# Moving score matmuls and probability products inside one attention step of an encoder kernel

## The chip, the cores and the metric

The kernel runs on one core of one Trainium2 chip. The metric is the device time of one execution in microseconds (us); a lower number is better. Engines are called by the names of the profile: PE (matrix multiply), PEld (its weight loads), DVE (vector), ACT (activations), POOL (GpSimd) and SP (which only issues transfers here).

## The reference

One encoder layer runs over two token sequences, a prompt of 512 tokens and a sample of 2048. The layer is a norm, an input projection, a mixer made of a pooling half and an attention half, an output projection, and a feed-forward part with a short convolution. Only the attention matters for this change:

```
def attend(q_blk):
    s = jnp.einsum('bqhd,bkhd->bhqk', q_blk, k_full).astype(jnp.float32) * scale
    p = jax.nn.softmax(s, axis=-1).astype(v.dtype)
    return jnp.einsum('bhqk,bkhd->bqhd', p, v)
```

There are 8 heads, 96 values in a query or key, 64 in a value, and no mask: every query sees every key of its own sequence.

## The kernel before, in words

The kernel first projects all tokens and leaves queries, keys and the pooled half in HBM, with the values in SBUF. Then comes the attention, then the output projection, and last the feed-forward part. All fp32 operands of matmuls are cut into two fp16 parts, a high and a low one.

The attention is a list of **units**. A unit is one head and one block of queries: 256 queries in the prompt (16 wide units, 0 to 15) and 128 queries in the sample (128 narrow units, 16 to 143). A narrow unit has 16 tiles of 128 keys, so its scores fill 4 PSUM banks of 512 columns, 4 tiles to a bank. Scores stand transposed, keys on the partitions. One narrow unit i goes through these pieces:

- `st_scores` (L935): 3 matmuls (high by high, high by low, low by high) for each key tile, 12 to a bank, 48 to a unit.
- `st_max` (L951): DVE reduces a bank over its 4 tiles to 128 columns; `st_fold` (L971) folds the results of the first three banks into one, and bank 3 has its own.
- `st_T` (L978): two PE transposes put the folded maximum and the maximum of bank 3 side by side in a PSUM tile called x, of which there is only one.
- `st_redT` (L991): DVE reduces x to the maximum of each query and cuts it in two parts (three instructions).
- `st_rep` (L1005): one more PE transpose into x, and ACT copies the negative to SBUF. This is **the copy of the maximum**, tile mr (L1013).
- `st_r1` (L1016): four matmuls of 512 columns add that negative maximum to the four banks.
- `st_exp` (L1030): ACT takes the exponential of each bank into pf (fp32).
- `st_hi` (L1037) casts pf to fp16 (ph), on ACT or on DVE; `st_lo` (L1051) lets POOL form the rest pl = pf - ph.
- `st_pv` (L1056): **the products**, 16 tiles with 2 matmuls each (ph of 129 columns, pl of 65 columns). Their output lies in the x tile of a later unit, so they can't start before that unit's copy of the maximum has left x, and x can't be written anew before the products' output has been copied away.
- `st_out` (L1073): ACT copies the products' output (L1082); `st_out2` (L1087) normalizes and stores once in four units.

The order on every engine is written out by hand. The program takes one step for each i, and a string of letters says which pieces the step issues. Each engine works through its own instructions in exactly that order, so a piece that waits holds up what stands behind it on its engine. The letters that matter: `r` adds the maximum to the banks of unit i, `e0` and `e1` are the exponentials of banks 0 to 2 and of bank 3, `A` and `B` the two halves of a unit's products, `o` the copy of their output, `L` the scores of bank 3 of unit i+1, `a b c` the scores of banks 0 to 2 of unit i+2, `x y z` their maxima, `F` the fold, `M` the maximum of bank 3 of unit i+1, `T`, `d` and `R` the three stages of the maximum of unit i+1 (transposes, reduction, transpose back with its copy), `h0 h1` casts on ACT, `f2 f3` casts on DVE, `l0` to `l3` the rests on POOL. Before the change:

```
A=lambda i: run(st_pv, i - 1, 0),
B=lambda i: run(st_pv, i - 2, 1),
h1=lambda i: run(st_hi, i, 1),
f2=lambda i: run(st_hi, i, 2, 0.5, dve),
f3=lambda i: run(st_hi, i, 2.5, 1.5, dve),
ORDER = "r e0 B L o e1 a M f2 T d b c h0 R h1 l0 l1 A x y f3 l2 l3 z F q"
```

So the first half of the products of unit i-1 stood behind `R`, and its second half at the head of the next step. The banks of scores come from a ring of seven PSUM banks (`bank`, L930); a bank comes free when the exponential of the unit that held it has been taken. From step 36 on, two steps of every four also issue a piece of `prep_w_out` (L818), which scales and cuts the weights of the output projection; two of these pieces go through the x tile on PE and DVE.

Of the kernel before, what the change touches and what calls it, by code (L numbers as in the profile page):

```python
# [48 lines left out]
def encoder(ctx, tc, ins, outs, seq_names=("x_prompt", "x_sample")):  # L49
    nc = tc.nc  # L50
    act, dve, pool, pe = nc.scalar, nc.vector, nc.gpsimd, nc.tensor
# [160 lines left out]
    with tp("wA", 1) as wA, tp("pA", 2) as pA, tc.manual_schedule():  # L212
# [142 lines left out]
        sg, _ = pow2_scale(amr[:, 0:4], 0)  # L355
# [12 lines left out]
        sw, _ = pow2_scale(amr[:, 4:5], 15)  # L368
# [97 lines left out]
        swu, _ = pow2_scale(amr[:, 5:6], 15)  # L466
# [217 lines left out]
        skv, _ = pow2_scale(amr[:, 6:8], 15)  # L684
        swk, swv = skv[:, 0:1], skv[:, 1:2]
        swp, _ = pow2_scale(amr[:, 10:11], 15)
# [6 lines left out]
        swq, _ = pow2_scale(qm, 15)  # L693
# [87 lines left out]
        k = NC - 1  # L781
# [31 lines left out]
    f2 = wC.tile([P, 8], F32, name="f2")  # L813
# [84 lines left out]
    with tp("pB", 2) as pB, tp("psX", 1, "right", space=PSUM) as psX, \  # L898
# [27 lines left out]
        state = {}  # L926
# [3 lines left out]
        def bank(name):  # L930

            nbank[0] += 1
            return (psS if nbank[0] % 7 else psT).tile([P, 512], F32, name=name, tag="st")

        def st_scores(i, b):  # L935
            u = units[i]
            s, h, w = u["s"], u["h"], u["w"]
            if u["first"] and b == 0:
                j = [x for x in range(len(heads)) if heads[x][0] is s and heads[x][1] == h][0]
                if j + 1 < len(heads) and j > 0:  # L940
                    load_head(*heads[j + 1])
            kt, qt = loaded[(s["base"], h)]
            st = u["st"][b] = bank(f"st_{i}_{b}")
            t0, t1 = u["banks"][b]
            for t in range(t0, t1):
                for n, (x, y) in enumerate(THREE):
                    pe.matmul(st[:, (t - t0) * w:(t - t0 + 1) * w], kt[:, x, t * P:(t + 1) * P],  # L947
                              qt[:, y, u["q0"]:u["q0"] + w], start=n == 0 and t == t0, stop=n == 2,
                              skip_group_check=True)
# [106 lines left out]
        def st_pv(i, part):  # L1056
            u = units[i]
            s, h, nq, nkt, w = u["s"], u["h"], u["nq"], u["nkt"], u["w"]
            if part == 0:
                op = state.get(("x", i + 2 if i >= wide - 1 else wide if i >= wide - 3 else NU)) or bank(f"op_{i}")  # L1060
                u["op"] = op[:, :2 * 129].rearrange("p (j c) -> p j c", j=2)
            op = u["op"]
            k0 = s["base"] // P
            jobs = [(j, t) for j in range(nq) for t in range(nkt)]
            n = len(jobs)
            parts = PARTS
            for j, t in jobs[parts[part] * n // 16:parts[part + 1] * n // 16]:
                c0 = t * w + j * P
                pe.matmul(op[:, j, 0:129], u["ph"][:, c0:c0 + P], V[:, k0 + t, h, 0:129], start=t == 0, stop=False)  # L1069
                pe.matmul(op[:, j, 64:129], u["pl"][:, c0:c0 + P], V[:, k0 + t, h, 64:129], start=False,  # L1070
                          stop=t == nkt - 1)

        def st_out(i):  # L1073
            u = units[i]
            s, h, nq, op = u["s"], u["h"], u["nq"], u["op"]
            qi = u["q0"] // P
            grp = qi // 4
            key = ("t", s["base"], h, grp)
            if key not in state:
                state[key] = pB.tile([P, 4, VW], F32, name=f"t_{i}", tag="tacc")  # L1080
            tt = state[key]
            act.activation(tt[:, qi % 4:qi % 4 + nq, 0:129], op[:, 0:nq, 0:129], AF.Copy)  # L1082
            if (qi + nq) % 4 == 0 or (qi + nq) * P == s["S"]:
                n = qi % 4 + nq
                pool.tensor_tensor(out=tt[:, :n, 64:128], in0=tt[:, :n, 64:128], in1=tt[:, :n, 0:64], op=ALU.add)
# [23 lines left out]

        NU = len(units)  # L1110
        prep = prep_w_out(pB, lambda: state["x", max(k for n, k in (x for x in state if x[0] == "x"))])
        PARTS = [0, 8, 16]
        wide = sum(u["nq"] > 1 for u in units)
        ps_first = {}

# [6 lines left out]
        def run(fn, k, *a):  # L1122
            if 0 <= k < NU:
                fn(k, *a)

        def some(fn, k, bs):
            if 0 <= k < NU:
                for b in bs:
                    if b < len(units[k]["banks"]):
                        fn(k, b)  # L1130

        step = dict(
            r=lambda i: some(st_r1, i, range(4)),
            e=lambda i: some(st_exp, i, range(4)),
            e0=lambda i: some(st_exp, i, range(3)),
            e1=lambda i: some(st_exp, i, [3]),
            A=lambda i: run(st_pv, i - 1, 0),
            B=lambda i: run(st_pv, i - 2, 1),
            E=lambda i: run(st_pv, i - 2, 0),
            L=lambda i: some(st_scores, i + 1, [3]),  # L1140
            a=lambda i: some(st_scores, i + 2, [0]),
            b=lambda i: some(st_scores, i + 2, [1]),
            c=lambda i: some(st_scores, i + 2, [2]),
            t=lambda i: some(st_scores, i + 3, [0]),
            u=lambda i: some(st_scores, i + 3, [1]),
            M=lambda i: some(st_max, i + 1, [3]),
            x=lambda i: some(st_max, i + 2, [0]),
            y=lambda i: some(st_max, i + 2, [1]),
            z=lambda i: some(st_max, i + 2, [2]),
            F=lambda i: run(st_fold, i + 2),  # L1150
            h0=lambda i: run(st_hi, i, 0),
            h1=lambda i: run(st_hi, i, 1),
            f1=lambda i: run(st_hi, i, 1, 1, dve),
            f2=lambda i: run(st_hi, i, 2, 0.5, dve),
            f3=lambda i: run(st_hi, i, 2.5, 1.5, dve),
            l0=lambda i: some(st_lo, i, [0]),
            l1=lambda i: some(st_lo, i, [1]),
            l2=lambda i: some(st_lo, i, [2]),
            l3=lambda i: some(st_lo, i, [3]),
            T=lambda i: run(st_T, i + 1),  # L1160
            d=lambda i: run(st_redT, i + 1),
            R=lambda i: run(st_rep, i + 1),
            o=lambda i: run(st_out, i - 2),
            q=lambda i: run(st_out2, i - 3))
        START = ["a b x y", "a b T d t x u y R", "r e T d t R x y u f1 l1 h0 l0",
                 "r e T d t R x y u f1 l1 h0 l0", "r e T d E B R x y f1 l1 h0 l0 o q"]
        ORDER2 = "r e E B o T d a b x R f1 l1 y h0 q l0 c z F"
        TURN = {wide - 1: "r e L a M x T d b h0 f1 R y l0 l1 E B o c z F q",
                wide: "r e0 E B L o e1 a M f2 T d b c h0 R h1 l0 l1 A x y f3 l2 l3 z F q"}
        ORDER = "r e0 B L o e1 a M f2 T d b c h0 R h1 l0 l1 A x y f3 l2 l3 z F q"  # L1170
        for i in range(-2, NU):
            order = START[i + 2] if i + 2 < len(START) else TURN.get(i, ORDER2 if i < wide else ORDER)
            for x in order.split():
                step[x](i)
            if i >= NU // 4 and i % 4 in (0, 1):
                next(prep, None)
            if i == NU - 8:
                for _ in prep:
                    pass
                c_load_m(0)  # L1180
                c_load_m(1)
        todo = [(0, 0), (0, 1), (1, 0), (1, 1), (0, 2), (1, 2), (0, 3), (1, 3)]
        st_pv(NU - 2, 1)
        st_pv(NU - 1, 0)
        st_out(NU - 2)
        st_pv(NU - 1, 1)
        st_out(NU - 1)
        for m in range(2):
            if m == 1:
                for mp in range(2):  # L1190
# [39 lines left out]
    h2, nxt = [], []  # L1230
# [318 lines left out]
    with tp("pG", 1) as pG, tc.manual_schedule():  # L1549
# [8 lines left out]
        for bi, (up, dn) in enumerate(blocks):  # L1558
            nb = len(up)
            rr = pE.tile([P, NF], F32, name=f"rr_{bi}", tag="rr")  # L1560
            for f in range(NF):
# [12 lines left out]
                for ci in range(len(gfs), nb):  # L1574
# [8 lines left out]
                    if ci == 0:  # L1583
                        imA = g_scale(bi, "A", 0, NF - 1, rr)
                        if bi == 0:
# [10 lines left out]
            o = 0  # L1596
# [9 lines left out]
            for ci, (s, a, n) in enumerate(dn):  # L1606
                t = pH.tile([P, NTM, D], F32, name=f"y_{bi}_{ci}", tag="hy")
# [4 lines left out]
            for d in range(KT):  # L1612
                w, dws = dws, []
                ysc = []
                for nm, im in (("A", imA), ("B", imB)):
                    y_ = pE.tile([P, 1], F32, name=f"ysc{nm}_{bi}_{d}", tag=f"ysc{nm}")
# [10 lines left out]
                for ci in range(nb):  # L1627
# [10 lines left out]
                    else:  # L1638
                        first = NF // 4 if dn[ci][2] > 256 else NF // 2
                        if not more:  # L1640
                            first = NF // 4 if dn[ci][2] > 256 and dn[ci - 1][2] <= 256 else NF // 7
# [88 lines left out]
```

## Time and profile before

| what | value |
|---|---|
| median of 3 runs | 3176.3 us (3175.12 to 3176.63) |
| the profiled execution's own time | 3171.86 us |
| its span in the profile | 3170.1 us |
| PE, DVE, ACT, POOL busy over the whole span | 96%, 68%, 44%, 27% |
| narrow units of the attention | from about 432 us to about 1185 us of the span |
| granted clock of PE over the execution | 0.991 of full speed |

The profile is of one execution. Times in its views are microseconds from the start of the span; each row of a timeline gives start, duration, engine, line, operation, tiles and count, and in brackets how long the engine had stood idle before and what ended that. Matmuls are pipelined: the next one starts before the one before has ended, so their pace is read from the starts.

### The profile page before, as it was taken

To read this page: it belongs to the slowest core of one execution; us is meant where nothing else is said; L and a number is where in the kernel's file an instruction comes from. 1 tells how busy PE (TensorE), PEld (TensorE's weight loads), DVE (VectorE), ACT (ScalarE), POOL (GpSimd) and SP (SyncE) were. 2 spreads that over 40 slices of the span, in tenths; PEclk is the share of its full clock that TensorE was granted. 3 is DMA by queue.
4 is the path that set the end of the run, shared out by engine and by line. 5 is a ranking of instruction groups with operands and counts; after the bars stand their busy time and mean duration, and the time that the engine had idled before them with its cause. 6 is when DMAs were issued, how large, how long until landed. Compare 5 with 4: busy or idle time off the path is not lost. (4 is left out here: it accounts for less than half of the span.)

```text
span 3170.1 us, 60582 instructions
## 1 busy us (share of the span) xinstructions
PE 3035.8 (96%) x24731; PEld 1943.4 (61%) x24731; DVE 2140.6 (68%) x4746; ACT 1403.3 (44%) x2991; POOL 856.8 (27%) x864
## 2 busy tenths in 40 slices
PE   6999889999999999999999999999999999999998
PEld 4777578888877874445555555555555555555554
DVE  6677788889988884347777777543366666664332
ACT  4555456666666663223333333333333333333333
POOL 2211378888878882220000000001100000000000
PEclk9999899999999999999999999999999999999999
DMA  3332221200111014572111112211431111112111
GB/s 137 102 115 89 75 57 35 72 22 13 29 22 35 2 35 159 203 225 78 41 40 41 41 41 65 90 38 42 105 103 40 41 40 41 41 59 90 37 44 72
DMA packets 272065, 210.41 MB, mean 66 GB/s; under 512 B 48739, under 2 KB 247722, under 8 KB 271530
## 3 DMA queue, kind: packets, MB, share of 16 engines
q1 hardware_dynamic: 270012, 200.23, 21.5%
q8 instruction: 194, 3.18, 0.4%
q0 software_dynamic: 1440, 5.24, 0.4%
q10 hardware_dynamic: 334, 1.06, 0.1%
q14 instruction: 85, 0.70, 0.1%
HBM read 140.51 MB, written 55.38 MB: 62 GB/s over the span
## 5 line engine op out<-in xcount | busy, mean ns | idle before, releaser
L1296 PE MATMUL up<-h,ws 128*128 128x512 f16 (+1 forms) x6336 | 1145.7, 344 | 5.4 <-DMA h<-h_x_sample 4.0
L1296 PEld LDWEIGHTS <-ws 128*128 128x128 f16 x6336 | 619.6, 98 | 531.1 <-issue 5.0
L1054 POOL TENSOR_TENSOR pl<-pf,ph 128x512 f16<-128x512 f32 x544 | 619.5, 1159 | 187.8 <-ACT ph L1049 88.4
L1395 PE MATMUL dn<-G,wds 128*128 128x512 f16 (+1 forms) x3168 | 579.0, 344 | 0.0
L1395 PEld LDWEIGHTS <-wds 128*128 128x128 f16 x3168 | 310.0, 98 | 254.2
L947 PE MATMUL st<-Q,K 96*128 96x128 f16 (+1 forms) x6336 | 415.6, 222 | 4.4 <-DVE ms_s L133 1.2
L947 PEld LDWEIGHTS <-K 96*128 96x128 f16 x6336 | 394.8, 100 | 22.2 <-issue 2.1
L1035 ACT ACTIVATE pf<-st,cs 128x512 f32<-128x512 f32 x544 | 346.4, 690 | 117.1 <-PE st L1022 115.5
L961 DVE TENSOR_REDUCE mx<-st 128x128 f32<-128x512 f32 x512 | 339.0, 683 | 50.1 <-PE st L947 49.3
L1301 ACT ACTIVATE c<-up,ctab 128x511 f32<-128x511 f32 (+3 forms) x264 | 182.1, 699 | 410.0 <-PE up L1296 403.7
L1302 DVE SCALAR_TENSOR_TENSOR c<-up,ctab,c 128x510 f32<-128x510 f32 (+3 forms) x264 | 173.6, 657 | 188.3 <-ACT c L1301 185.4
L1069 PE MATMUL x<-V,ph 128*128 128x129 f16 x2040 | 212.9, 221 | 49.3 <-ACT mr L1013 46.7
L1070 PEld LDWEIGHTS <-pl 128*128 128x128 f16 x2176 | 194.0, 98 | 75.2 <-POOL pl L1054 69.0
L1069 PEld LDWEIGHTS <-ph 128*128 128x128 f16 x2176 | 195.4, 98 | 34.9 <-issue 34.6
L1070 PE MATMUL x<-V,pl 128*128 128x65 f16 x2040 | 204.9, 193 | 0.0
L1047 DVE TENSOR_REDUCE ph<-pf 128x256 f16<-128x256 f32 (+2 forms) x272 | 183.6, 675 | 3.4 <-ACT pf L1035 3.4
L1402 DVE SCALAR_TENSOR_TENSOR yt<-dn,yscB,yt 128x512 f32<-128x512 f32 (+1 forms) x48 | 31.5, 659 | 226.7 <-ACT yt L1401 216.9
L1305 DVE SCALAR_TENSOR_TENSOR c<-up,ctab,c 128x511 f32<-128x511 f32 (+1 forms) x264 | 174.7, 662 | 9.3
L1049 ACT ACTIVATE ph<-pf 128x512 f16<-128x512 f32 x272 | 173.2, 637 | 0.0
L128 ACT ACTIVATE ws<-wr,sF 128x1024 f16<-128x1024 f32 x88 | 96.2, 1138 | 145.5 <-DVE sF L1273 141.5
L1343 POOL PARTITION_ALL_REDUCE imrA<-imxA x2 | 0.7, 374 | 578.1 <-DVE imxA L1341 578.1
L1270 POOL PARTITION_ALL_REDUCE war<-wam x22 | 7.8, 356 | 526.5 <-DVE wam L1268 520.1
(413 smaller groups left out, 3606.0 us busy)
## 6 DMA issues: line engine op xcount, KB each, us to landing
wr<-in_w_up SPq DMA_DIRECT2D x88, 512.0 KB, 4.8
wd<-in_w_down SPq DMA_DIRECT2D x32, 512.0 KB, 4.1
x_s<-in_x_sample SPq DMA_DIRECT2D x8, 1024.0 KB
xt_Cs<-in_x_sample SPq DMA_DIRECT2D x8, 1024.0 KB, 7.5
x_x_sample<-xt_Cs SPq DMA_DIRECT2D x8, 1024.0 KB, 3.9
h_x_sample<-rows_Cs SPq DMA_DIRECT2D x16, 512.0 KB, 2.6
wd<-in_w_down SPq DMA_DIRECT2D x16, 384.0 KB, 3.4
y<-x_x_sample SPq DMA_DIRECT2D x3, 2048.0 KB, 8.9
```

The lines of the kernel that those rows point to most:

```text
L947: pe.matmul(st[:, (t - t0) * w:(t - t0 + 1) * w], kt[:, x, t * P:(t + 1) * P], qt[:, y, u["q0"]:u["q0"] + w], start=n == 0 and t == t0, st ...
L961: dve.tensor_reduce(u["mx2"] if b == 3 else u["mx3"][:, :, b], st.rearrange("p (t q) -> p q t", q=w), axis=AX.X, op=ALU.max)
L1035: act.activation(u["pf"][:, c], u["st"][b][:, :c.stop - c.start], AF.Exp, scale=cs[:, 0:1])
L1047: dve.tensor_reduce(u["ph"][:, c], u["pf"][:, c].rearrange("p (c o) -> p c o", o=1), axis=AX.X, op=ALU.max)
L1054: pool.tensor_tensor(out=u["pl"][:, c], in0=u["pf"][:, c], in1=u["ph"][:, c], op=ALU.subtract)
L1069: pe.matmul(op[:, j, 0:129], u["ph"][:, c0:c0 + P], V[:, k0 + t, h, 0:129], start=t == 0, stop=False)
L1070: pe.matmul(op[:, j, 64:129], u["pl"][:, c0:c0 + P], V[:, k0 + t, h, 64:129], start=False, stop=t == nkt - 1)
L1296: pe.matmul(ps[:, :ncol], ws[side][:, k, x, :], ht[:, k, y, :ncol], start=m == 0, stop=m == 3 * KT - 1)
L1301: act.activation(c[:, :n], ps[:, :n], AF.Identity, scale=cw[:, 1, col:col + 1], bias=ctab[:, 3, col:col + 1])
L1302: dve.scalar_tensor_tensor(out=c[:, 1:n], in0=ps[:, 0:n - 1], scalar=cw[:, 0, col:col + 1], in1=c[:, 1:n], op0=ALU.mult, op1=ALU.add)
L1305: dve.scalar_tensor_tensor(out=c[:, 0:j1], in0=ps[:, 1:1 + j1], scalar=cw[:, 2, col:col + 1], in1=c[:, 0:j1], op0=ALU.mult, op1=ALU.add)
L1395: pe.matmul(acc[part][:, :n], w[f // 8][:, f % 8, x, :], G_[0][:, f, y, o:o + n], start=f in (0, NF - 1) and (x, y) == (0, 0), stop=f >= N ...
```

## The change

Only the order is changed, and the pieces are cut differently; no arithmetic is added or left out. In a narrow step the products of a unit are both issued two steps later (`A` now takes unit i-2, as `B` did), with 9 of the 16 tiles in `A` and 7 in `B`, around `L`. Behind `R` now stand the scores of three of the four tiles of bank 2 of unit i+2 (`c1`); the fourth tile (`c2`) comes in the next step behind `r`, and its maximum and the fold (`z1`, `F1`) with it. Bank 0 is cut in two halves (`a1`, `a2`) around the transposes `T`. Of the casts, DVE now takes bank 2 in one instruction of 512 columns (`f2`), and ACT takes banks 0 and 1 in one of 1024 columns (`h2`) and bank 3 in one of 512 (`h3`).

```diff
-        def st_scores(i, b):
+        def st_scores(i, b, j0=0, j1=4):
...
-            st = u["st"][b] = bank(f"st_{i}_{b}")
+            if j0 == 0:
+                u["st"][b] = bank(f"st_{i}_{b}")
+            st = u["st"][b]
             t0, t1 = u["banks"][b]
-            for t in range(t0, t1):
+            for t in range(t0 + j0, min(t0 + j1, t1)):
...
-                op = state.get(("x", i + 2 if i >= wide - 1 else wide if i >= wide - 3 else NU)) or bank(f"op_{i}")
+                op = state["x", i + 2] if wide - 3 <= i < NU - 2 else bank(f"op_{i}")
...
-        PARTS = [0, 8, 16]
+        PARTS = [0, 9, 16]
...
-            A=lambda i: run(st_pv, i - 1, 0),
+            A=lambda i: run(st_pv, i - 2, 0),
             B=lambda i: run(st_pv, i - 2, 1),
-            E=lambda i: run(st_pv, i - 2, 0),
+            a1=lambda i: some(st_scores, i + 2, [0], 0, 2),
+            a2=lambda i: some(st_scores, i + 2, [0], 2, 4),
+            c1=lambda i: some(st_scores, i + 2, [2], 0, 3),
+            c2=lambda i: some(st_scores, i + 1, [2], 3, 4),
+            z1=lambda i: some(st_max, i + 1, [2]),
+            F1=lambda i: run(st_fold, i + 1),
...
-            h1=lambda i: run(st_hi, i, 1),
+            h2=lambda i: run(st_hi, i, 0, 2),
+            h3=lambda i: run(st_hi, i, 3),
             f1=lambda i: run(st_hi, i, 1, 1, dve),
-            f2=lambda i: run(st_hi, i, 2, 0.5, dve),
-            f3=lambda i: run(st_hi, i, 2.5, 1.5, dve),
+            f2=lambda i: run(st_hi, i, 2, 1, dve),
...
-        ORDER2 = "r e E B o T d a b x R f1 l1 y h0 q l0 c z F"
-        TURN = {wide - 1: "r e L a M x T d b h0 f1 R y l0 l1 E B o c z F q",
-                wide: "r e0 E B L o e1 a M f2 T d b c h0 R h1 l0 l1 A x y f3 l2 l3 z F q"}
-        ORDER = "r e0 B L o e1 a M f2 T d b c h0 R h1 l0 l1 A x y f3 l2 l3 z F q"
+        ORDER2 = "r e A B o T d a b x R f1 l1 y h0 q l0 c z F"
+        TURN = "r e A B o L a M x T d b h0 f1 R y l0 l1 c1 q"
+        ORDER = "r e0 c2 A L B o e1 z1 F1 M f2 a1 T a2 d b h2 R h3 c1 x y l2 l0 l1 l3 q"
...
-        st_pv(NU - 2, 1)
-        st_pv(NU - 1, 0)
-        st_out(NU - 2)
-        st_pv(NU - 1, 1)
-        st_out(NU - 1)
+        for k in (NU - 2, NU - 1):
+            for part in range(2):
+                st_pv(k, part)
+            st_out(k)
```

The wide units keep their order (`E` and the new `A` are the same piece there), apart from the one step at the turn to narrow units. The last two units' products move behind the last step.

PE, around the transpose back (`R`) in the step of unit 80. x_81 is the x tile of unit 81, p3 what is transposed, ph_79 and pl_79 the probabilities of unit 79, st_82_2 bank 2 of unit 82. Before:

```order
L947 LDWEIGHTS K_512_4_11084
L947 MATMUL st_82_2_13352<-Q_512_4_11085,K_512_4_11084 128x128
L1010 MATMUL x_81_13333<-ident_60,p3_4272 128x128
L1069 LDWEIGHTS ph_79_13209
L1069 MATMUL x_81_13333<-V_88,ph_79_13209 128x129
L1070 LDWEIGHTS pl_79_13210
L1070 MATMUL x_81_13333<-V_88,pl_79_13210 128x65
```

And with the change:

```order
L949 LDWEIGHTS K_512_4_11043
L949 MATMUL st_82_1_13275<-Q_512_4_11044,K_512_4_11043 128x128
L1012 MATMUL x_81_13263<-ident_60,p3_4272 128x128
L949 LDWEIGHTS K_512_4_11043
L949 MATMUL st_82_2_13293<-Q_512_4_11044,K_512_4_11043 128x128
```

Eight pairs of products, which write into the tile that the copy reads, gave their place behind the transpose to nine score matmuls, which write into a bank of their own.

DVE, from the maximum of bank 3 of unit 81 (mx2_81) back and onward. mx3 takes the maxima of banks 0 to 2, ph_80 is written by the casts. Before:

```order
L1047 TENSOR_REDUCE ph_79_13209<-pf_79_13159 128x768
L961 TENSOR_REDUCE mx3_81_13267<-st_81_2_13231 128x128
L976 TENSOR_REDUCE mx_81_13274<-mx3_81_13267 128x128
L961 TENSOR_REDUCE mx2_81_13328<-st_81_3_13300 128x128
L1047 TENSOR_REDUCE ph_80_13330<-pf_80_13280 128x256
L996 TENSOR_REDUCE x_81_13333<-x_81_13333 128x1
```

And with the change:

```order
L963 TENSOR_REDUCE mx3_81_13183<-st_81_1_13155 128x128
L963 TENSOR_REDUCE mx3_81_13183<-st_81_2_13173 128x128
L978 TENSOR_REDUCE mx_81_13249<-mx3_81_13183 128x128
L963 TENSOR_REDUCE mx2_81_13251<-st_81_3_13219 128x128
L1049 TENSOR_REDUCE ph_80_13253<-pf_80_13194 128x512
L998 TENSOR_REDUCE x_81_13263<-x_81_13263 128x1
```

The cast of 768 columns is gone from DVE, and the one that stands between the maximum of bank 3 and the reduction of x has 512 columns where it had 256.

ACT, from the exponentials of unit 80 to the copy of the maximum of unit 81 (mr2_81); t_76 takes the products' output. Before:

```order
L1035 ACTIVATE pf_80_13280<-st_80_2_13106,cs_1165 128x512
L1082 ACTIVATE t_76_13059<-x_80_13212 128x129
L1035 ACTIVATE pf_80_13280<-st_80_3_13179,cs_1165 128x512
L1049 ACTIVATE ph_80_13330<-pf_80_13280 128x512
L1013 ACTIVATE mr2_81_13367<-x_81_13333 128x128
```

And with the change:

```order
L1037 ACTIVATE pf_80_13194<-st_80_2_13049,cs_1165 128x512
L1084 ACTIVATE t_76_12994<-x_80_13143 128x129
L1037 ACTIVATE pf_80_13194<-st_80_3_13099,cs_1165 128x512
L1051 ACTIVATE ph_80_13253<-pf_80_13194 128x1024
L1015 ACTIVATE mr2_81_13290<-x_81_13263 128x128
```

The cast ahead of the copy of the maximum doubled in length; nothing else changed its place in this stretch.

## Rows read from the trace of the kernel before

**Rows 1.** Busy time by stretch: all narrow units (us, busy, instructions, clock).
```profile
432.00:1185.00 753.00, 699.17 (x11011) 602.69 (x11011) 667.31 (x1350) 498.83 (x1025) 616.86 (x571) 1.00 0.11 28
```
**Rows 2.** The copy of the maximum alone, 432 to 1186 us.
```profile
L1013 ACT ACTIVATE mr<-x x127: 277/277/278, 438.2 to 1184.7; 128x128 fp32r<-128x128 f32 x127
...
  PE x L1069: 46.4, 127
```
**Rows 3.** Timeline of one step, PE (and one weight load, PEld).
```profile
903.96 0.51 PE L1022 MATMUL st<-mr,ones 2*128 2x512 f32 x4
...
904.39 0.23 PE L1069 MATMUL x<-V,ph 128*128 128x129 f16 x1
...
905.28 1.50 PE L947 MATMUL st<-Q,K 96*128 96x128 f16 x24
...
906.62 0.61 PE L988 MATMUL x<-ident,mx 128*128 128x128 f32 x2
...
906.89 0.14 PEld L988 LDWEIGHTS x<-ident,mx 128*128 128x128 f32 x1 [0.15 <-DVE mx L961]
...
907.06 1.50 PE L947 MATMUL st<-Q,K 96*128 96x128 f16 x24
...
908.40 0.28 PE L1010 MATMUL x<-ident,p 128*128 128x128 f32 x1
...
909.05 0.22 PE L1069 MATMUL x<-V,ph 128*128 128x129 f16 x1 [0.36 <-ACT mr L1013]
...
909.71 0.19 PE L1070 MATMUL x<-V,pl 128*128 128x65 f16 x1
...
909.84 0.50 PE L1022 MATMUL st<-mr,ones 2*128 2x512 f32 x4
```
**Rows 4.** The same step, ACT.
```profile
904.54 1.84 ACT L1035 ACTIVATE pf<-st,cs 128x512 f32<-128x512 f32 x3 [0.91 <-PE st L1022]
...
906.27 0.29 ACT L1082 ACTIVATE t<-x 128x129 f32<-128x129 f32 x1
906.42 0.70 ACT L1035 ACTIVATE pf<-st,cs 128x512 f32<-128x512 f32 x1
...
906.99 0.65 ACT L1049 ACTIVATE ph<-pf 128x512 f16<-128x512 f32 x1
...
908.72 0.28 ACT L1013 ACTIVATE mr<-x 128x128 fp32r<-128x128 f32 x1 [1.07 <-PE x L1010]
```
**Rows 5.** The same step, DVE.
```profile
906.15 0.69 DVE L961 TENSOR_REDUCE mx<-st 128x128 f32<-128x512 f32 x1 [0.51 <-PE st L947]
...
906.75 0.41 DVE L1047 TENSOR_REDUCE ph<-pf 128x256 f16<-128x256 f32 x1
...
907.33 0.43 DVE L996 TENSOR_REDUCE x<-x 128x1 f32<-128x256 f32 x1 [0.17 <-PE x L988]
...
909.39 0.94 DVE L1047 TENSOR_REDUCE ph<-pf 128x768 f16<-128x768 f32 x1
...
910.25 0.68 DVE L961 TENSOR_REDUCE mx<-st 128x128 f32<-128x512 f32 x1
...
910.97 0.55 DVE L976 TENSOR_REDUCE mx<-mx 128x128 f32<-128x384 f32 x1
```
**Rows 6.** The page's costliest groups: a cast of 1024 columns, and the rests on POOL.
```profile
L1054 POOL TENSOR_TENSOR pl<-pf,ph 128x512 f16<-128x512 f32 x544 | 619.5, 1159 | 187.8 <-ACT ph L1049 88.4
...
L128 ACT ACTIVATE ws<-wr,sF 128x1024 f16<-128x1024 f32 x88 | 96.2, 1138 | 145.5 <-DVE sF L1273 141.5
```
**Rows 7.** Timeline of one step with a piece of the weights' preparation through x.
```profile
941.18 0.22 PE L1069 MATMUL x<-V,ph 128*128 128x129 f16 x1 [1.32 <-DVE m L840]
...
942.28 2.72 PE L947 MATMUL st<-Q,K 96*128 96x128 f16 x24
```
**Rows 8.** Timeline of a step with a cut of the weights on ACT.
```profile
1008.86 0.50 ACT L128 ACTIVATE w_o<-w_o,f 128x256 f16<-128x256 f32 x1
```
**Rows 9.** The same stretch, DVE.
```profile
1010.88 0.71 DVE L133 SCALAR_TENSOR_TENSOR w_o<-w_o,f 128x256 f16<-128x256 f32 x1
```

More of the change, by code (lines that the diff above doesn't have):

```diff
@@ L933, in bank @@
             return (psS if nbank[0] % 7 else psT).tile([P, 512], F32, name=name, tag="st")
-        def st_scores(i, b):
+        def st_scores(i, b, j0=0, j1=4):
             u = units[i]
             s, h, w = u["s"], u["h"], u["w"]
-            if u["first"] and b == 0:
+            if u["first"] and b == 0 and j0 == 0:
                 j = [x for x in range(len(heads)) if heads[x][0] is s and heads[x][1] == h][0]
@@ L1124, in run, with some @@
                 fn(k, *a)
-        def some(fn, k, bs):
+        def some(fn, k, bs, *a):
             if 0 <= k < NU:
@@ L1129, in some @@
                     if b < len(units[k]["banks"]):
-                        fn(k, b)
+                        fn(k, b, *a)
         step = dict(
@@ L1165, in encoder @@
         START = ["a b x y", "a b T d t x u y R", "r e T d t R x y u f1 l1 h0 l0",
-                 "r e T d t R x y u f1 l1 h0 l0", "r e T d E B R x y f1 l1 h0 l0 o q"]
-        ORDER2 = "r e E B o T d a b x R f1 l1 y h0 q l0 c z F"
-        TURN = {wide - 1: "r e L a M x T d b h0 f1 R y l0 l1 E B o c z F q",
-                wide: "r e0 E B L o e1 a M f2 T d b c h0 R h1 l0 l1 A x y f3 l2 l3 z F q"}
-        ORDER = "r e0 B L o e1 a M f2 T d b c h0 R h1 l0 l1 A x y f3 l2 l3 z F q"
+                 "r e T d t R x y u f1 l1 h0 l0", "r e T d A B R x y f1 l1 h0 l0 o q"]
+        ORDER2 = "r e A B o T d a b x R f1 l1 y h0 q l0 c z F"
+        TURN = "r e A B o L a M x T d b h0 f1 R y l0 l1 c1 q"
+        ORDER = "r e0 c2 A L B o e1 z1 F1 M f2 a1 T a2 d b h2 R h3 c1 x y l2 l0 l1 l3 q"
         for i in range(-2, NU):
-            order = START[i + 2] if i + 2 < len(START) else TURN.get(i, ORDER2 if i < wide else ORDER)
+            order = START[i + 2] if i + 2 < len(START) else ORDER2 if i < wide - 1 else TURN if i < wide else ORDER
             for x in order.split():
```

## The prediction

> **What bounds the kernel now.** [...] Nobody is idle enough to look like the waiting party, so the next view is one instruction that occurs once a unit, the copy of the maximum: 127 copies lie between 438.2 and 1184.7 us, and PE waited for them 46.4 us in all, 0.37 us at each [rows 2]. The timeline of one step gives the rest. From one `r` to the next is 909.84 - 903.96 = 5.88 us [rows 3]; 126 such steps make 740.9 us, and the 5.6 us that are left of 746.5 belong to a few steps, below. The reader is to follow one loop through [rows 3 to 5], with `r` at 0: products B at 0.43, scores L at 1.32, maximum M on DVE at 2.19, reduction of x at 3.37, R at 4.44, the copy on ACT at 4.76, products A at 5.09, `r` at 5.88. Each link waits for the one before: L starts at 905.28 because the first exponential, which frees its bank, ends at 904.54 + 0.69 [rows 3, 4]; the second transpose waits 0.15 for M [rows 3]; A waits for the copy, since it writes the tile that the copy reads. So a narrow unit is bound by this loop, no engine's work. In it A is pure length: it needs the copy, then stands 0.79 ahead of `r`, which needs only the copy. (A last fact: 0.1 us a step is 12.6 us in all.)
>
> **The change, part by part.** All on the clock of one step, `r` at 0; prices are paces from starts.
>
> Scores: 24 take 906.62 - 905.28 = 1.34 [rows 3], 0.056 each, 0.67 a bank. Products: from 909.05 the sixteenth starts at 909.71 [rows 3], so 0.044 each, 0.088 a pair; with the turn to the next weights eight pairs take up to 0.79, 0.099 a pair, which I keep as upper end.
>
> - c2, three scores behind `r`: 0.43 to 0.60. It puts z1 on DVE at about 0.80 instead of at the end of the step before.
> - A, nine pairs: 0.60 to 1.39. No wait: the copy that frees x was awaited by `r` already, and POOL's rests belong to a unit two steps back.
> - L: 1.39 to 2.06. The first exponential ends at 0.58 + 0.69 = 1.27 [rows 3, 4], so the wait for the bank goes.
> - M comes 0.20 after L's last issue, as now (905.95 to 906.15) [rows 3, 5]: 2.26. On DVE z1 (0.68) and F1 (0.55) [rows 5] are done at about 2.05, so they are hidden, with 0.2 to spare.
> - B, seven pairs: 2.06 to 2.68. a1, six scores: to 3.02.
> - The copy of the products' output, `o`, must follow B now, and T must follow `o`, for there is one x tile. Nothing in the trace shows this lag in a narrow step; the nearest rows are 0.20 from L to M and 0.32 from R to its copy [rows 3 to 5]. B ends with a short matmul, so I take 0.20: `o` 2.88 to 3.17, T at 3.23 (0.06 behind, as 906.56 to 906.62) [rows 3, 4]. **This is the wait that takes the removed one's place: PE stands about 0.2 before T.**
> - T to reduction: 0.71 now, less the 0.15 that T waited for M [rows 3, 5], which is done at 2.95: 0.56, so 3.79. The cast f2 stands between M and the reduction on DVE. It starts 0.60 after M, at 2.86; 256 columns took 0.41 and 768 took 0.94 [rows 5], so 512 take 0.675: done at 3.54, 0.25 early.
> - Reduction to R: 1.07 [rows 3, 5], R at 4.86. PE: T's 0.44 [rows 3], a2 0.34, b 0.67, done at 4.68, waits 0.2.
> - R to copy 0.32, copy to the waiting PE 0.33 [rows 3, 4]: `r` at 5.51. Under it c1, nine scores: R takes (0.44 - 0.15) / 2 = 0.15, so 5.01 to 5.51. Both end together: **the next step starts at 5.51**, 0.37 earlier than now.
>
> On ACT the copy queues behind the long cast h2: e1 0.15 behind `o`, h2 0.57 behind that [rows 4], 3.60, and 1024 columns took 1.14 [rows 6]: 4.74, and the copy is due at 5.18. 0.44 to spare. h3, 0.65 [rows 4], ends around 6.0, before the next exponentials at 5.51 + 0.58. POOL: four rests of 1.16 [rows 6] are 4.64 of 5.51, and they have a whole step more until they are read; in order behind f2, h2, h3 the last ends near 8.2, and is due near 13. DVE loses 0.68 a step (0.41 + 0.94 becomes 0.675); no end hangs on it, so I count nothing.
>
> The scores' weights and DMAs: the load of the next head is issued with a1 where it was issued with `a`, behind L as before; no queue of SP or POOL is passed. No gain, no loss.
>
> Sum over 126 steps: 126 x 0.37 = 46.6 us. The odd steps: two pieces of the weights' preparation pass through x, and PE waited 1.32 for DVE, with the next 24 scores at 2.72 instead of 1.34 [rows 7]; most of the 5.6 us is there, because that DVE piece stood behind z and F. Now it stands ahead of z1, read at about 0.8 where A is due at 0.60: I take 4 us back. Against it stand the eight cuts of weights, 0.50 on ACT ahead of the exponentials [rows 8] and 0.71 on DVE ahead of z1 [rows 9], which now have 0.1 to 0.2 of cover: up to 0.3 each, 2 us. The wide units keep their order, and behind the last step the products wait for POOL's last rest as now: 0, within 2 either way. Together 48.6 us. The profiled execution took 3171.9 us, which becomes 3123.3; the median shown is 4.4 us above it, so 3127.7: **3128 us**.
>
> [...] The pace of c1 decides whether it hides under the copy; the rows say 0.056 a score [rows 3]. [...]
>
> **The rivals.**
> 1. *The nine scores outlast the copy.* Between two waits a short run may go slower than 24 in a row. For it: c1 has no slack. Against it: 0.056 in every full-pace stretch. The slowest pace in the trace is 2.72 / 24 = 0.113 [rows 7]; half way to it, 0.085, gives 5.01 + 0.77 = 5.78, or 126 x 0.10 + 2 = 15 us: 3162. Chance 0.08.
> 2. *DVE is late.* z1, F1, M and f2 all stand ahead of the reduction now, where 0.41 stood. If M comes 0.4 late, f2 ends at 3.94, the reduction starts 0.19 late, and the step is 5.70: 126 x 0.18 + 2 = 25 us, 3152. Against it: 0.2 ahead of M and 0.25 ahead of the reduction to spare. Chance 0.08.
> 3. *`o` comes sooner*, 0.1 behind B and the products at their best pace: T at 3.10, step 5.38 (c1 must follow by then, and b ends early enough): 126 x 0.50 + 2 = 65 us, 3111. Chance 0.08.
> 4. *The wait only moves.* With products at 0.099 (B ends 0.18 later) and `o` 0.32 behind, T is 0.30 later: 5.81. With 0.07 more nothing is gained: about 3176, no change. Chance 0.05.
> 5. *Slower, through the one x tile.* B, `o` and T are a new chain through PE, ACT and PE inside the loop, and T's delay counts fully. From 0.37 on, `o` costs more than the change brings; at 0.5, if `o` waits behind ACT's exponentials or B for a rest on POOL, the step is 6.01 and the kernel loses 126 x 0.13 = 16 us: 3193. Against it: the three exponentials end at 0.58 + 1.84 = 2.42 [rows 4], before B does. Chance 0.05.
>
> **How the numbers follow.** The forecast itself has 0.66; its own ends are lags and paces: steps of 5.42 to 5.60, 3117 to 3139. The range reaches down to rival 3 with a little below it (0.03 left out) and up through rival 2; outside at the top are most of rival 1 (0.06) and rivals 4 and 5 (0.10). That gives 3108 to 3156 with 0.19 left out. A change of 0.2%, 6.4 us, is about what a measurement of this kernel can tell. Forecast and rivals 1 to 3 are faster: 0.90; rival 4 is the same: 0.05; rival 5 is slower: 0.05.
>
> **What would show it.** In the profile after: copies of the maximum 5.4 to 5.6 us apart; PE no longer waiting for the copy ahead of products; a new short wait of T for `o`, near 0.2; the reduction 0.56 behind T, with f2 over; ACT still idle ahead of the copy, by 0.4. It is wrong if the copies stand 5.8 us or more apart; then `o`'s lag behind B, or the end of c1 against the end of the copy, tells which rival it was. If the steps shrink and the time does not, the wide units or the end took it back.

## The result, and the profile after

The changed kernel takes 3126.7 us (median of 4 runs, 3125.64 to 3130.14) where the kernel before takes 3175.71 (4 runs): a ratio of 0.9845, 95% interval 0.9832 to 0.9858. The forecast was 3128 us. The span of the profiled execution fell from 3170.1 to 3123.9 us, by 46.2.

The busy times by stretch over the narrow units, with the same columns as [rows 1]:

```profile
432.00:1140.00 708.00, 685.01 (x11002) 591.66 (x11003) 606.33 (x1227) 567.03 (x1025) 615.08 (x573) 1.00 0.12 30
```

The narrow units now take 708 us instead of 753. PE is busy 685 of them, 97% where it was 93%; DVE's busy time fell by 61 us (the second cast is gone), that of ACT rose by 68, above all by the casts it took over, and POOL is where it was.

The copy of the maximum, its count, first and last start, and who waited for it (answers to [rows 2]):

```profile
L1015 ACT ACTIVATE mr<-x x128: 277/278/278, 432.8 to 1139.2; 128x128 fp32r<-128x128 f32 x128
...
  PE x L1012: 62.8, 128
...
  PEld st L1024: 0.6, 1
```

Products don't wait for the copy any more (46.4 us before), and `r`, which needs it, waited for it once. (The row `PE x L1012` is the copy's own wait for PE.) In a stretch without odd steps the copies stand this far apart:

```profile
L1015 ACT ACTIVATE mr<-x x14: 277/278/278, 487.8 to 559.8; 128x128 fp32r<-128x128 f32 x14
```

72.0 us for 13 steps are 5.54 us a step, where it was 5.88. A step like these, which carries no piece of the weights' preparation, is called plain below. One step in the timeline, PE with two weight loads (answers to [rows 3]):

```profile
875.50 0.51 PE L1024 MATMUL st<-mr,ones 2*128 2x512 f32 x4
...
875.94 0.34 PE L949 MATMUL st<-Q,K 96*128 96x128 f16 x3
...
876.90 0.83 PE L949 MATMUL st<-Q,K 96*128 96x128 f16 x12
...
878.19 0.50 PE L949 MATMUL st<-Q,K 96*128 96x128 f16 x6
...
878.72 0.20 PEld L990 LDWEIGHTS x<-ident,mx 128*128 128x128 f32 x2 [0.21 <-ACT t L1084]
878.72 0.44 PE L990 MATMUL x<-ident,mx 128*128 128x128 f32 x2
...
880.27 0.14 PEld L1012 LDWEIGHTS x<-ident,p 128*128 128x128 f32 x1 [0.28 <-DVE p L1004]
880.28 0.33 PE L1012 MATMUL x<-ident,p 128*128 128x128 f32 x1
...
880.44 0.67 PE L949 MATMUL st<-Q,K 96*128 96x128 f16 x9
880.64 0.28 ACT L1015 ACTIVATE mr<-x 128x128 fp32r<-128x128 f32 x1 [0.45 <-PE x L1012]
...
881.04 0.51 PE L1024 MATMUL st<-mr,ones 2*128 2x512 f32 x4
```

The same step on ACT and then on DVE (answers to [rows 4, 5]):

```profile
876.09 1.84 ACT L1037 ACTIVATE pf<-st,cs 128x512 f32<-128x512 f32 x3 [0.20 <-PE st L1024]
878.39 0.28 ACT L1084 ACTIVATE t<-x 128x129 f32<-128x129 f32 x1 [0.45 <-PE x L1072]
878.57 0.68 ACT L1037 ACTIVATE pf<-st,cs 128x512 f32<-128x512 f32 x1
879.14 1.06 ACT L1051 ACTIVATE ph<-pf 128x1024 f16<-128x1024 f32 x1
```

```profile
877.78 0.69 DVE L963 TENSOR_REDUCE mx<-st 128x128 f32<-128x512 f32 x1 [0.18 <-PE st L949]
878.38 0.68 DVE L1049 TENSOR_REDUCE ph<-pf 128x512 f16<-128x512 f32 x1
879.27 0.43 DVE L998 TENSOR_REDUCE x<-x 128x1 f32<-128x256 f32 x1 [0.21 <-ACT pf L1037]
```

Read with `r` at 0, the places of the prediction and of this step stand side by side:

| place | predicted | measured |
|---|---|---|
| c2 behind `r` | 0.43 | 0.44 |
| L | 1.39 | 1.40 |
| M | 2.26 | 2.28 |
| a1 | 2.68 | 2.69 |
| f2 on DVE | 2.86 | 2.88 |
| `o`, copy of the products' output | 2.88 | 2.89 |
| T, behind `o` | 3.23 | 3.22 |
| reduction of x | 3.79 | 3.77 |
| R | 4.86 | 4.78 |
| c1 | 5.01 | 4.94 |
| copy of the maximum | 5.18 | 5.14 |
| next `r` | 5.51 | 5.54 |

The two new waits of PE are in the brackets: 0.21 for `o` ahead of T, 0.28 for DVE ahead of R. The wait that the view gives for the reduction names an exponential on ACT, whose end (879.25) lies close by chance; by the starts it is T, 0.55 ahead, as predicted: in each of the 14 steps between 485 and 560 us the reduction starts 0.38 behind the second transpose, and f2 had been over for 0.2.

### The profile page after: what moved, and what is told of

It is laid out like the page before. It is cut to its first block, busy times and chain, and to the rows that moved or that the text cites. A ratio compares the mean times of both kernels' runs of the same rounds, so it can differ in the third digit from the quotient of the medians.

```text
span 3123.9 us, 60357 instructions
## 1 busy us (share of the span) xinstructions
PE 3019.2 (97%) x24731; PEld 1932.9 (62%) x24731; DVE 2076.8 (66%) x4618; ACT 1472.1 (47%) x2991; POOL 854.6 (27%) x864
## 3 DMA queue, kind: packets, MB, share of 16 engines
q10 hardware_dynamic: 334, 1.06, 0.1%
## 5 line engine op out<-in xcount | busy, mean ns | idle before, releaser
L949 PE MATMUL st<-Q,K 96*128 96x128 f16 (+1 forms) x6336 | 478.0, 222 | 1.6 <-DVE ms_s L133 1.2
L1051 ACT ACTIVATE ph<-pf 128x512 f16<-128x512 f32 (+1 forms) x272 | 224.8, 827 | 0.0
L1428 POOL TENSOR_TENSOR y<-y,fng 128x512 f32<-128x512 f32 (+1 forms) x42 | 45.5, 1086 | 384.3 <-ACT yp L1419 356.2
```

The lines of the kernel that those rows point to most:

```text
L1051: act.activation(u["ph"][:, c], u["pf"][:, c], AF.Copy)
```

## The experiments

All of these put pieces in another order or cut them elsewhere, and compute the same thing. The first five are single runs. Ahead of the narrow units and behind them, where their orders are the change's but for one step at the turn, their profiles differ from the change's by up to 4 and 7 us, so their argument rests on the step and less on the total. The others are medians of four. The step of a kernel is read as above, first to last copy of the maximum between 485 and 560 us over their count less one.

**One: the casts back.**

```diff
-            f2=lambda i: run(st_hi, i, 2, 1, dve),
+            f2=lambda i: run(st_hi, i, 2, 0.5, dve),
+            f3=lambda i: run(st_hi, i, 2.5, 1.5, dve),
+            h1=lambda i: run(st_hi, i, 1),
...
-        ORDER = "r e0 c2 A L B o e1 z1 F1 M f2 a1 T a2 d b h2 R h3 c1 x y l2 l0 l1 l3 q"
+        ORDER = "r e0 c2 A L B o e1 z1 F1 M f2 a1 T a2 d b h0 R h1 c1 x y f3 l0 l1 l2 l3 q"
```

> The changed order on PE, but the casts as before: DVE takes 256 and 768 columns of banks 2 and 3, ACT one bank each side of the copy. Theory (the loop through PE, ACT and DVE sets the step; the casts only lie in its shade): the cast of 768 goes between y and z1, M starts about 0.2 us later, still ahead of the second transpose; plain steps 5.53 to 5.60 us, with 24 steps that carry a piece of the weights' preparation some 0.4 us longer because DVE then has no cover; 3130 to 3142 us. Rival (the relief of DVE by 0.68 us a step carries the gain): steps of 5.75 us or more, 3155 us or more.

Measured: 3140.9 us, beside 3177.7 for the kernel before on the same chip. A plain step takes 5.54 us, exactly the change's:

```profile
L1015 ACT ACTIVATE mr<-x x14: 277/277/278, 485.6 to 557.6; 128x128 fp32r<-128x128 f32 x14
```

So the regrouped casts shorten no plain step; there the relief of DVE is worth nothing. They are worth some 9 us (715.6 us from the first to the last copy of the narrow units, where the change takes 706.3) in the steps that carry a piece of the weights' preparation, most of which take 5.76 to 5.97 us here, because DVE then has no gap left to hide the piece in: around one such piece it works from 662.8 to 667.6 us without a pause. The other 5 us of the difference between the totals lie ahead of and behind the narrow units, where the two kernels have the same order.

**Two: the products alone.** The order before, with both halves of the products moved two units back and nothing put under the copy; old casts. The line is shown against the kernel before.

```diff
-        ORDER = "r e0 B L o e1 a M f2 T d b c h0 R h1 l0 l1 A x y f3 l2 l3 z F q"
+        ORDER = "r e0 A B L o e1 a M f2 T d b c h0 R h1 l0 l1 x y f3 l2 l3 z F q"
```

> The order before with one part of the change alone: both halves of the products two units back, at the head of the step ahead of L; the scores of bank 2 whole and ahead of R as before, nothing under the copy of the maximum, old casts. Theory: the loop loses the 0.79 us of A between the copy and r, gains 0.70 of A ahead of L and loses the 0.15 to 0.2 that L waited for its bank: a step of about 5.61 us, and PE stands about 0.5 us behind R in every step; 3140 to 3146 us. Rival (the scores under the copy carry the gain): 5.85 us or more, 3172 us or more.

Measured: 3153.2 us; the step is 5.62 (67.4 us in 12), as expected. The total missed its range by 7 us, and not for the plain steps: most steps with a piece of the preparation take 5.71 to 5.91, and the two that pass through x take 7.87 and 9.36. Together the odd steps cost 6.6 us more than in the kernel before; another 6.5 us were lost behind the narrow units, where the order is the change's. In a plain step `r` now waits for the copy, as the waits of this kernel between 485 and 560 us show (us in total, times, longest):

```profile
PEld st L1024 <- ACT mr L1015: 7.3, 13, 0.6
```

So taking the products out of the stretch between the copy and `r` gives 0.26 of the 0.34 us, and it does so though PE stands idle there. The other 0.08 comes from the rest of the change together; no run takes it apart.

**Three: both halves ahead of L.**

```diff
-        ORDER = "r e0 c2 A L B o e1 z1 F1 M f2 a1 T a2 d b h2 R h3 c1 x y l2 l0 l1 l3 q"
+        ORDER = "r e0 c2 A B L o e1 z1 F1 M f2 a1 T a2 d b h2 R h3 c1 x y l2 l0 l1 l3 q"
```

> The change with both halves of the products ahead of L instead of around it. Theory: M comes 0.62 us later, at 2.88, and f2 stands behind it on DVE, done at 4.16, so the reduction starts at about 4.2 instead of 3.76: a step of 5.95 us (5.83 if f2 did not hold it), 3165 to 3182 us. Rival (it matters only that the products left the copy's shade, not where they went): 5.53 us, 3127 us.

Measured: 3167.5 us, a step of 5.84 (70.1 us in 12), and not 5.95. It equals the value named for the case that f2 does not hold the reduction, but by luck: f2 does hold it, by less than expected. In the step from 702.56 the reduction starts at 706.64, right behind f2 (706.05, 0.68 long) and 0.46 behind the second transpose, where it is 0.38 in the change; from `r` that is 4.08 instead of 4.2. The wait of T moved to where the theory has it, from the copy `o` to the maximum M (waits of this kernel, same stretch and columns):

```profile
PEld x L990 <- DVE mx L963: 6.3, 12, 0.5
```

Where the products went decides: ahead of L, they give back nearly all. L must come early enough for M, and B fits behind it because only `o` waits for B.

**Four, five: bank 2 cut twelve and none, six and six.** In the change nine scores stand under the copy and three at the head of the next step.

```diff
-            c1=lambda i: some(st_scores, i + 2, [2], 0, 3),
-            c2=lambda i: some(st_scores, i + 1, [2], 3, 4),
+            c1=lambda i: some(st_scores, i + 2, [2]),
...
-            c1=lambda i: some(st_scores, i + 2, [2], 0, 3),
-            c2=lambda i: some(st_scores, i + 1, [2], 3, 4),
+            c1=lambda i: some(st_scores, i + 2, [2], 0, 2),
+            c2=lambda i: some(st_scores, i + 1, [2], 2, 4),
```

The first of these two leaves `c2` out of the step's order.

> The change with bank 2 whole under the copy: 12 scores in c1, no c2 at the head of the next step. Theory: the head gets 0.17 us shorter and everything behind it comes 0.17 earlier, up to R; then the twelve scores (0.67 and a turn to other weights of 0.1) and no longer the copy end last, 0.92 behind R: a step of 5.52 us, 3125 to 3129 us, no change. Rival (the copy sets the next r in the change, and scores in its shade cost nothing): R and r both 0.17 earlier, 5.36 us, 3106 us. Rival (the longer stretch pushes the loop): 5.70 us, 3148 us.

Measured for twelve: 3143.2 us, a step of 5.63 (67.6 us in 12). That is between the theory and the second rival: L wanted to start at 1.22, but its bank comes free at 1.3: in the step from 701.37 the first exponential ends at 702.64 and L starts at 702.70, 1.33 behind `r` where it was 1.40. So the head got only 0.07 shorter instead of 0.17, while the twelve scores lasted 0.17 longer. I had left that wait out of the expectation.

> The change with bank 2 cut two and two: six scores under the copy, six at the head of the next step. Theory: T and R 0.17 later (3.38 and 4.94); six scores end at 5.44 and leave the copy to end last: r at 5.64, 3140 us. Rival (the next r follows the end of c1 alone): 5.54 us, 3127 us.

Measured for six: 3138.3 us, a step of 5.63 (67.6 us in 12), as expected. Who held `r` is in the waits between 485 and 560 us: with six scores under the copy, `r` waits for the copy in each of the 13 steps; with twelve there is no such row, nor with nine. The row of the kernel with six:

```profile
PEld st L1024 <- ACT mr L1015: 2.6, 13, 0.2
```

So in the change the last of the nine scores, and not the copy, ends the step: the timeline has c1 at 880.44, its ninth score at 880.89, and `r` at 881.04, 0.15 behind that where the next score would have stood 0.056 behind, while the copy was over at 880.92. Rival 1 of the prediction holds in small: the nine scores outlast the copy, though by this turn of 0.10 and not by a slower pace.

**Six, seven: the scores cut to fit the waits.** If the loop runs as claimed, three scores at the head are dear and scores ahead of T and R, where PE waits 0.21 and 0.28, are free.

```diff
-            a1=lambda i: some(st_scores, i + 2, [0], 0, 2),
-            a2=lambda i: some(st_scores, i + 2, [0], 2, 4),
-            c1=lambda i: some(st_scores, i + 2, [2], 0, 3),
-            c2=lambda i: some(st_scores, i + 1, [2], 3, 4),
+            a1=lambda i: some(st_scores, i + 2, [0], 0, 3),
+            a2=lambda i: some(st_scores, i + 2, [0], 3, 4),
+            c0=lambda i: some(st_scores, i + 2, [2], 0, 1),
+            c1=lambda i: some(st_scores, i + 2, [2], 1, 4),
...
-        PARTS = [0, 9, 16]
+        PARTS = [0, 10, 16]
...
-        TURN = "r e A B o L a M x T d b h0 f1 R y l0 l1 c1 q"
-        ORDER = "r e0 c2 A L B o e1 z1 F1 M f2 a1 T a2 d b h2 R h3 c1 x y l2 l0 l1 l3 q"
+        TURN = "r e A B o L a M x T d b h0 f1 R y l0 l1 c q"
+        ORDER = "r e0 A L B o e1 z1 F1 M f2 a1 T a2 d b h2 c0 R h3 c1 x y l2 l0 l1 l3 q"
```

> The change with its scores cut to fit the waits: bank 0 in three tiles ahead of T and one behind it, bank 2 wholly in one step, one tile ahead of R and three under the copy, nothing at the head; products 10 and 6 tiles so that L finds its bank free. Theory (in the change the loop runs from r through A, L, B, the copy of their output, T, the reduction and R to the last score of c1 and a turn of 0.1): the head loses c2's 0.17, T comes at 3.07, R at 4.63, c1 ends at 5.29: a step of 5.39 us, 3107 to 3112 us. Rival (the odd tile ahead of R or the longer A holds R or M back): 5.50 us or more, no change against the change's 3127 us.

Measured: 3107.7 us (4 runs; ratio to the kernel before 0.9799, 0.9784 to 0.9814), a step of 5.38 (69.9 us in 13).

The next kernel has two tiles in `c0` and two in `c1`.

> As the kernel that fits the scores to the waits, but with two tiles of bank 2 ahead of R and two under the copy. Theory: the scores ahead of R end at 4.64, just when R is due; c1 is over at 5.23 and the copy ends last: a step of 5.33 to 5.37 us, 3101 to 3109 us. Rival (PE is full between T and R): R later by a tile's 0.1 to 0.17, 5.45 us, 3116 us.

Measured: 3100.2 us (4 runs; 0.9774, 0.9759 to 0.9789), a step of 5.30 (68.9 us in 13), a little under the forecast. PE no longer waits ahead of T or R, and now the copy does end last, as the timeline of one step shows:

```profile
704.21 0.33 PE L1012 MATMUL x<-ident,p 128*128 128x128 f32 x1
...
704.38 0.50 PE L949 MATMUL st<-Q,K 96*128 96x128 f16 x6
704.58 0.28 ACT L1015 ACTIVATE mr<-x 128x128 fp32r<-128x128 f32 x1 [0.45 <-PE x L1012]
...
704.90 0.19 PEld L1024 LDWEIGHTS st<-mr,ones 2*128 2x128 f32 x4 [0.20 <-ACT mr L1015]
```

The change itself, timed beside these two:

> The change itself once more, on the same chip as the kernels with the scores cut otherwise: 5.53 us a step and 3124 to 3130 us.

Measured: 3125.5 us (4 runs; 0.9853, 0.9836 to 0.9869). Its interval touches neither of the two others'; those two overlap a little, their runs (3105.0 to 3111.2 and 3098.6 to 3101.0) do not, and their steps of 5.38 and 5.30 agree with that.

**Eight: the cuts of the weights, moved.** The steps that carry a cut cost more than predicted, and the cut's half on DVE lasted 0.96 or 1.31 us where it had lasted 0.71 [rows 9]. This experiment starts from the kernel with two tiles ahead of R; `cut` is the half on DVE, put off to stand behind M of the next step.

```diff
-            split(w_o_part(m, 0)[:, c], w_o_part(m, 1)[:, c], w_o[:, m + 1, c], f2[:, m:m + 1])
+            hi, lo, src, sc = w_o_part(m, 0)[:, c], w_o_part(m, 1)[:, c], w_o[:, m + 1, c], f2[:, m:m + 1]
+            act.activation(hi, src, AF.Identity, scale=sc)
...
+            if n == 4:
+                cuts.append(cut)
...
                 step[x](i)
+                if x == "M" and cuts:
+                    cuts.pop(0)()
```

> As the kernel with two tiles ahead of R, but the DVE half of each of the eight early cuts of the output projection's weights is issued one step later, just behind M, where POOL stands idle until f2 is done; the ACT half stays. Theory (an instruction of DVE with two inputs in SBUF takes turns with POOL: in the change and in the kernel before, each of these cuts ends 0.28 us after the POOL instruction that runs when it starts, whether that makes it 0.71, 0.96 or 1.31 us): the cuts take 0.28 to 0.45 us each, the steps with a cut 5.55 to 5.70 us instead of 5.92 and 6.20, 3094 to 3099 us. Rival (the cut is long for its own sake, or from waiting for ACT's half): 0.7 us or more each as before, the steps with a cut 5.9 us or more, 3100 us or more.

Measured: 3095.2 us (4 runs; ratio to the kernel before 0.9752, 0.9731 to 0.9773), the lowest of all. Its interval overlaps that of experiment seven, so the narrow units decide, 676.4 us from their first to their last copy where it was 679.7. Seven of the cuts, in the groups between 880 and 990 us:

```profile
L862 DVE SCALAR_TENSOR_TENSOR w_o<-w_o,f 128x256 f16<-128x256 f32 x7 | 3.3, 476 | 0.0
```

They take 0.48 us, a little over the 0.28 to 0.45 named, and the steps with a cut take 5.65 us, within the range, where they took 5.92 and 6.20. The theory of turns between DVE and POOL was borne out in this, and the rival (0.7 us or more) was not; the rows are in the last section.

## Why the prediction was right

**The loop.** The reading of the bottleneck held: a step is bound by the loop through `r`, L, M or `o`, T, the reduction, R and what follows R. Experiments two, five, six and seven move the step by what its links say (5.61 expected and 5.62 measured; 5.64 and 5.63; 5.39 and 5.38; 5.33 to 5.37 and 5.30). Experiments three and four move it the way expected or show why not, but miss in size (5.95 and 5.84; 5.52 and 5.63), each at a link that the expectation had mis-sized or left out. Experiment one, which gives DVE its 0.68 us of casts back, changes no plain step.

**The new wait.** T behind `o` was the claimed successor of the removed wait; it is there, 0.21 us. The unseen lag from B to `o` was taken as 0.20, the shorter of the two rows, and it is 0.20 (878.19 to 878.39): `o` started at 2.89 against 2.88. That it is the shorter because B ends with a short matmul was not tried.

**Two terms were mis-sized, against each other.** From the reduction to R I counted 1.07 [rows 3, 5]; it is 1.01 (879.27 to 880.28). In the kernel before, PE was itself busy with scores up to R, so that row held some of PE's own time: R stood 0.12 behind the end of DVE's last piece there and stands 0.06 behind it here. And I let `r` follow the ninth score of c1 at once, 5.51, though I knew a turn to other weights from the products; it takes 0.10. The first error is 0.06 of the 0.08 by which R was forecast too late, the second forecast `r` 0.10 too early, and a step of 5.51 became 5.54. That the step was off by only 0.03 is thus in part luck.

**ACT and POOL.** The long cast took 1.06 instead of 1.14 and ended at 880.20, 0.44 ahead of the copy, as forecast. POOL held nobody in a plain step.

**The odd steps.** Predicted: 4 us back and 2 us lost. The two pieces through x now cost 0.13 and 0.06 us over a plain step, where they cost 2.69 and 2.57 (copies 8.57 and 8.45 us apart before): 5.1 back. About 1.2 of the 2.69 was not the wait itself but a slower pace of the scores behind it, which the prediction did not see. Behind the wait of 1.32 us [rows 7] the 24 scores start 107 ns apart, where those of [rows 3] start 56 apart. In this row of the kernel before, with the columns of [rows 1], the granted clock is 0.76; it is 0.50 from 942 to 944 us, in the midst of these scores, and 1.00 from 948 to 956:

```profile
942.00:948.00 6.00, 5.63 (x77) 5.37 (x75) 3.62 (x8) 2.17 (x5) 1.97 (x3) 0.76 0.00 0
```

So the 0.113 a score that the prediction gave rival 1 as the slowest pace was read where the granted clock was 0.50 (and 2.72 counts the last score to its end, where 1.34 counts starts). In the change PE does not wait there, and the granted clock is 1.00 (904 to 910 us). DVE reads x at 908.98 to 909.25 in the first of them, and the products start at 909.43, on time:

```profile
908.98 0.27 DVE L840 TENSOR_REDUCE m<-x 1x1 f32<-1x128 f32 x1
```

That the piece's place on DVE decides, behind `f3`, z and F or ahead of z1, is borne out by experiment two, which keeps the old place and pays 2.3 and 3.7 us. But the place ahead of z1 is not enough: in experiment one, where the cast `f3` still stands ahead of the piece, PE waits 0.56 and 0.53 us for DVE, and the two steps take 6.38 and 6.81. The eight cuts cost 0.31 to 0.67 each, 3.9 in all instead of 2: the term that I had sized only by the cover ahead of M, not by the cut's own length.

**The rest.** 126 plain steps by 0.35 are 44.1 us; with 1.3 from the odd steps, 1.2 from the first narrow step (6.55 to 5.31), 0.7 at the end of the attention, and less 1.1 lost before the first narrow unit (kernels with the same order there differ by up to 4), that is the 46.2 us of the span. The forecast had 48.6, and it put the median 4.4 above the profiled execution, where it is 1.1 above (3126.7 and 3125.64). The two errors cancel, so that the total came within 1.3 us is in part luck. The pace of c1, on which its place under the copy hung, came as counted: its nine scores are issued in about 0.5 us, 56 ns each, between two waits and all.

**The rivals.** Rival 1 came true in small, by a turn of 0.10 behind the ninth score. Rival 2 (DVE late) can be excluded: f2 was over 0.21 before the reduction began. Rivals 4 and 5 needed T 0.30 to 0.50 later than forecast; it came at 3.22 against 3.23. Rival 3, shorter than forecast, needed `o` 0.1 behind B; it came 0.20 behind, but the same step length came by another way, in experiment six.

## What to carry to other kernels

When a wait in a hand-ordered loop is to be filled, first ask which pieces lie on the loop, not which engine is idle: moving the products out of the stretch between the copy and its consumer gave 0.26 us even with nothing in their place, and where they went instead decided whether it lasted. Then write down the times of the new step, link by link, with the waits that it leaves; here its length was right to 0.03 us, with two errors against each other, and the two waits that it showed ahead of T and R were the places for the scores that the change had left at the head of the step, worth 25 us more. Work that occurs in few steps needs its own line, since cover that a tighter loop takes away is paid for there.

## What was not expected of the hardware

The cut of the weights on DVE, an instruction with two inputs in SBUF (128 by 256), took 0.71 to 1.31 us beside POOL's instructions and 0.48 in experiment eight. The POOL instruction that runs when one of them starts, in the timeline of the kernel before:

```profile
1010.15 1.16 POOL L1054 TENSOR_TENSOR pl<-pf,ph 128x512 f16<-128x512 f32 x1
```

The cut of [rows 9] ends at 1010.88 + 0.71 = 1011.59, 0.28 behind the end of that POOL instruction, 1011.31. In the change, two more POOL instructions of that kind:

```profile
931.68 1.16 POOL L1056 TENSOR_TENSOR pl<-pf,ph 128x512 f16<-128x512 f32 x1
...
948.59 1.16 POOL L1056 TENSOR_TENSOR pl<-pf,ph 128x512 f16<-128x512 f32 x1
```

And the cuts on DVE that start while they run, in the change's timeline:

```profile
931.81 1.31 DVE L133 SCALAR_TENSOR_TENSOR w_o<-w_o,f 128x256 f16<-128x256 f32 x1 [0.46 <-ACT w_o L128]
...
949.07 0.96 DVE L133 SCALAR_TENSOR_TENSOR w_o<-w_o,f 128x256 f16<-128x256 f32 x1 [0.45 <-ACT w_o L128]
```

931.81 + 1.31 is 0.28 behind 932.84, and 949.07 + 0.96 is 0.28 behind 949.75. All eight cuts of either kernel end 0.28 behind, whether their half on ACT had ended 0.03 or 1.5 us before they start. The POOL instruction that follows is longer too, 1.34 us instead of 1.16 in all 16 cases, as in the change's timeline:

```profile
949.70 1.34 POOL L1056 TENSOR_TENSOR pl<-pf,ph 128x512 f16<-128x512 f32 x1
```

So in these 16 cases the cut ended 0.28 us behind the POOL instruction that was there first, and the next one took 0.18 longer. The same instruction on DVE took 0.71, 0.96 or 1.31 us by where in POOL's instruction it happened to start. In experiment eight, where it stands behind M, seven of them took 0.48 on average; one starts 0.08 ahead of the end of POOL's instruction (912.06), and POOL then stands idle until 913.14:

```profile
911.98 0.48 DVE L862 SCALAR_TENSOR_TENSOR w_o<-w_o,f 128x256 f16<-128x256 f32 x1
```

The rows show the size: up to 0.83 us on a DVE instruction of 0.48 beside POOL instructions of 1.16. The casts, which have one input, did not change beside POOL: in the change those of 512 columns took 0.67 to 0.69 us, 37 of them with POOL idle and 91 wholly or partly beside it. That the second input makes this difference was not tried.
